# A trunk of two layers: seven products of halved blocks in the first feed-forward too, two weight sums by adding loads, and w_down steps between the products

## The chip, the cores and the metric

The kernel runs on one core of a Trainium2 chip. The core has a matrix engine (TensorE, in the profile PE, with its weight loads as PEld), VectorE (DVE), ScalarE (ACT), GpSimd (POOL) and SyncE (SP), and 16 DMA engines that all queues share. The metric is device time of one execution in microseconds; of several executions the median is given.

## The reference

A trunk of two layers over 512 latent tokens of 1024 channels, after a prefix of 256 context tokens. The even layer mixes by retention and convolution, the odd one by pooling and spatial gating; each is followed by a feed-forward. Before every part stands an RMSNorm with a shift and a scale, and behind it a gated residual; shift, scale and gate come from the vector `c` times `ada_w`. What matters here:

```python
def swiglu(h, w_gate, w_up, w_down):
    return (jax.nn.silu(h @ w_gate) * (h @ w_up)) @ w_down

D_MODEL, SEQ, DEPTH = 1024, 512, 2
D_FF = 2816            # 22 tiles of 128
# ada_w (DEPTH, 1024, 6 * 1024), ffn_w_gate and ffn_w_up (DEPTH, 1024, 2816), ffn_w_down (DEPTH, 2816, 1024)
```

All of it is float32.

## The kernel before

**Layout.** The residual stream stays in SBUF as eight tiles `xT[k]` of 128 channels x 512 tokens. A float32 product is made of three matmuls on rounded parts (`mm3`, L503): every operand is split into a high part (a rounding copy by ScalarE) and a low part (the operand minus the high part). For weights the low part is a subtraction on VectorE, or, for names in `DL`, a negated copy on ScalarE to which a DMA from GpSimd's queue then adds the operand (`low_part`, L413, `add_dma`, L327). Weight operands are 128 x 128, moving operands 512 columns (all tokens) or 256.

**First feed-forward** (`ffn`, L1596, called with layer 0). The 22 hidden tiles go in pieces of 8, 6, 4 and 4. For each four tiles `gemm` loads weights 0.5 MB at a time, splits them and makes gate and up in the straight form: per tile 8 blocks of rows x 3 matmuls of 512 columns. `gemm_acc` then adds the piece's product with w_down to `xT`, half of the output tiles at a time. The first four gate tiles are made while the norm before is still in work, and the last four rows of w_down are left to the stage that follows (`cross`, `last_of`), where they are multiplied half of the tokens at a time, so that the next norm can begin on the first half.

**Conditioning rows.** Beside the first feed-forward VectorE makes the modulation vectors of the rest: `ada` (L750) loads 0.5 MB of `ada_w`, into three buffers, and `row_dot` (L746) multiplies it with the vector and sums along the row. 56 of these are spread by `pace` over the stage, at a rate `ADA_RATE` of TensorE's time.

**Second feed-forward** (`ffn_seven`, L1762). Tiles 0 to 5 go in the straight form, tiles 6 to 21 in four groups of four. A group's gate is one product of a 1024 x 512 weight block with a 1024 x 512 block of `h`. Both are halved in both directions, and `seven` makes the four blocks of the result out of seven products instead of eight, each of 2 tiles x 4 blocks of rows x 3 = 24 matmuls of 256 columns (L1834); up is made in the same way. For that, sums of weight quarters are needed (`combine`, here four sums of two VectorE instructions in each group) and sums of quarters of `h` (`blocks`, once). The partial results lie in four PSUM banks a group: a second product is added to a bank after its first value was read by ScalarE or VectorE. High and low parts of gate times up are made by `rows_of` in tiles of the pool gp.

**Order.** In the second feed-forward the order on TensorE, VectorE and ScalarE is written out by hand: `steps` is a list, and each step's matmuls are followed by its evictions, then by the preparation of the weights that are used five steps later (`line.ahead(m + DEPTH)`), then by an entry of `filler` (the quarters of `h`, `rows_of`). An entry `(None, ...)` in `steps` puts the group's `rows_of` into `filler`. `Line` holds the weight loads in six buffers; a buffer is loaded anew on SP's queue when its last preparation was made. The product with w_down stands, for the first three groups, between the gate and the up of the group that follows, and for the last after its `(None, ...)` entry, with four output tiles at a time. In the first feed-forward the order is left to the scheduler, by priority.

Of the kernel before, what the change touches and what calls it, by code (L numbers as in the profile page):

```python
# [9 lines left out]
F32 = mybir.dt.float32  # L10
# [5 lines left out]
P = 128  # L16
D = 1024
# [12 lines left out]
ADA_RATE = 0.25  # L30
# [10 lines left out]
ACT_SLOTS = 46  # L41
# [13 lines left out]
WAY_V = ("extra", "extra", None, None)  # L55
# [12 lines left out]
PIECES = (8, 6, 4, 4)  # L68
# [3 lines left out]
FILLS = (0, 1, 1, 0, 1, 1, 1, 1, 2, 2, 2)  # L72
# [175 lines left out]
def trunk_kernel(ctx: ExitStack, tc: tile.TileContext, A, out: bass.AP):  # L248
# [104 lines left out]
    dump = const.tile([P, D], BF16, name="dump")  # L353
# [349 lines left out]
    def cross(w, k0, rhs, gate, name, order, scales, head, prep, func, end=lambda: None):  # L703

        W = [load_w(w, k0, 4, c0, 512, name) for c0 in (0, 512)]
# [38 lines left out]
    araw = [None]  # L744

    def row_dot(raw, row, dst, last=True):  # L746

        STT(out=raw if last else dump, in0=raw, scalar=1.0, in1=row, op0=ALU.mult, op1=ALU.mult, accum_out=dst)

    def ada(l, m):  # L750
# [16 lines left out]
        return [(1.2, piece(d)) for d in range(KD)]  # L767

# [37 lines left out]
    def even_start(pool):  # L806

        w_in = A["even_w_in"]

# [687 lines left out]
    def odd_layer(dpool, hx):  # L1497
# [89 lines left out]
        gemm_acc(A["odd_w_out"], 0, 4, pool_cat, mods[(1, 2)], 'oa')  # L1587
        a = scale_vec(mods[(1, 4)], 1, 1)
        sg = [slot() for _ in range(4)]
        order = [(A["ffn_w_gate"][1], 2 * b * P, 0, "f", WAY_F[b]) for b in range(4)]  # L1590
        h = cross(A["odd_w_out"], 4, sg_cat, mods[(1, 2)], 'ol', order, lambda: (a, mods[(1, 3)]),
                  lambda V, c, h: gate_half(V["f"], sg)(c, h), PREP_F, AF.Silu)
        return h, sg


    def ffn(l, begun, end):  # L1596
        wg, wu, wd = A["ffn_w_gate"][l], A["ffn_w_up"][l], A["ffn_w_down"][l]
        h, sg0 = begun
        g5 = mods[(l, 5)]
        f0 = 0  # L1600
        for nf in PIECES:
            G = []
            for fa in range(0, nf, 4):
                nt = min(4, nf - fa)
                c0 = (f0 + fa) * P
                sg = sg0 if c0 == 0 else [slot() for _ in range(nt)]

                def ev_gate(i, ps, c=slice(0, T)):
                    ACT(out=sg[i][:, c], in_=ps, func=AF.Silu)

                def ev_up(i, ps):
                    TT(out=sg[i], in0=ps, in1=sg[i], op=ALU.mult)
                    G.append(split(sg[i]))

                if c0:
                    gemm(wg, KD, c0, nt, h, ev_gate, name=f'g{l}')
                gemm(wu, KD, c0, nt, h, ev_up, name=f'u{l}' if c0 else f'v{l}')
            if f0 + nf < DFF // P:
                gemm_acc(wd, f0, nf, G, g5, f'd{l}')
            else:  # L1620
                return end(wd, f0, G, g5, f'l{l}')
            f0 += nf


    class Line:
# [4 lines left out]
        def __init__(self, pool):  # L1630
            self.pool = pool
            self.loads, self.last, self.raws = [], [], []
            self.preps, self.made, self.summed = [], [], 0
            self.q = {}

        def load(self, key, w, r0, rows, c0, cn):
            self.loads.append((key, w, r0, rows, c0, cn))
            self.last.append(None)
            return len(self.loads) - 1

        def fetch(self):

            while len(self.raws) < len(self.loads):
                n = len(self.raws)
                if n >= self.RAWS and self.last[n - self.RAWS] >= len(self.made):
                    return
                key, w, r0, rows, c0, cn = self.loads[n]
# [3 lines left out]
                nc.sync.dma_start(out=raw[:, :rows * cn].rearrange("p (k c) -> p k c", c=cn),  # L1651
                                  in_=w[r0 * P:(r0 + rows) * P, c0:c0 + cn].rearrange("(k p) c -> p k c", p=P))
                self.raws.append(raw)
                self.q[key] = [raw[:, x:x + T] for x in range(0, rows * cn, T)]

        def prep(self, key, uses, sums=None):

            n = len(self.preps)
            for u in uses:
                self.last[u] = n  # L1660
            self.preps.append((key, sums))
            return n
# [8 lines left out]
        def ahead(self, n):  # L1671

            while len(self.made) < min(n, len(self.preps)):
# [4 lines left out]
                for i, x in enumerate(src):  # L1678
                    ACT(out=hi[:, i * T:(i + 1) * T], in_=x, func=AF.Copy)
                for i, x in enumerate(src):  # L1680
                    c = slice(i * T, (i + 1) * T)
                    TT(out=lo[:, c], in0=x, in1=hi[:, c].bitcast(F32), op=ALU.subtract)
# [3 lines left out]
    def combine(a, b, op, out=None):  # L1686
        out = out or [slot() for _ in a]
        for o, x, y in zip(out, a, b):
            TT(out=o, in0=x, in1=y, op=op)
        return out  # L1690

    def blocks(h, pool):
# [16 lines left out]
        def sub(out, a, b):  # L1709
            def f():  # L1710
                o, x, y = ([t[:, :T], t[:, T:]] for t in (F[out], F[a], F[b]))
                combine(x, y, ALU.subtract, o)
# [9 lines left out]

        return B, [quarter("11", 0, n1), quarter("12", 0, n2), sub("11", "12", "11"), quarter("22", 1, n2),
                   sub("12", "22", "12"), sub("22", "22", "11"), both("t2", "22"), both("t1", "11"),
                   quarter("21", 1, n1), sub("21", "21", "22"), both("t3", "12"), both("t4", "21")]

    class Gate:
# [12 lines left out]
        def put(self, i, j, ps, sb=None):  # L1740
# [3 lines left out]
            else:  # L1744
                TT(out=o, in0=self.view(ps), in1=self.view(sb), op=ALU.add)
                self.later.append(lambda: ACT(out=o, in_=o, func=AF.Silu))

    class Up:
# [5 lines left out]
        def put(self, i, j, ps, sb=None):  # L1754
# [5 lines left out]
            TT(out=o, in0=self.g.view(ps), in1=o, op=ALU.mult)  # L1760

    def ffn_seven(l, begun, end, pool):  # L1762
# [138 lines left out]
        for nt in SEVENS:  # L1901
# [13 lines left out]
            if done:  # L1915
                down(*done)
# [152 lines left out]
```

## Time and profile before

| | us |
|---|---|
| median of 3 runs | 1129.09 |
| lowest and highest | 1128.79, 1129.55 |
| the profiled execution | 1128.8 |
| its span, from first to last instruction | 1126.8 |

The profile is that of one execution. The time of an execution is its span and what lies around it, here 2.0 us. Comparisons of a changed kernel are made with runs of the kernel before on the same chip.

### The profile page before, as it was taken

How to read it: one execution, taken by the hardware profiler on the slowest of the kernel's cores; microseconds unless marked ns; L12 is line 12 of the kernel's file. 1: busy time of each engine (PE TensorE's matmuls, PEld its weight loads, DVE VectorE, ACT ScalarE, POOL GpSimd, SP SyncE). 2: the span in 40 equal slices, each digit the busy share in tenths (PEclk: the TensorE clock that was granted, in tenths of full speed). 3: DMA queues.
4: the chain of work that ended last, by engine and by line, in shares of the span. 5: the costliest groups of instructions: out<-in, count | busy, mean ns of one | idle time of the engine just before them, and what ended most of it. 6: DMA issues, size and time to landing. Idle time of an engine off the chain costs nothing.

```text
span 1126.8 us, 15718 instructions
## 1 busy us (share of the span) xinstructions
PE 1104.3 (98%) x5978; PEld 943.8 (84%) x5978; DVE 827.0 (73%) x1472; ACT 474.5 (42%) x795; POOL 75.6 (7%) x104
## 2 busy tenths in 40 slices
PE   6999999999999999999999999999999999999997
PEld 3878876469988888888888988899889998989986
DVE  5989998998864655655653878567577886969856
ACT  5556655566522212322213543445334353524521
POOL 4012122313000000000000000000000000000000
PEclk7999999999999999999999999999999999999998
DMA  9689977569375666566534143233313252323302
GB/s 349 235 225 261 262 187 181 163 206 231 108 254 198 209 198 205 192 200 219 174 94 133 36 138 114 94 95 103 123 57 112 76 150 72 117 74 113 113 1 75
DMA packets 88827, 173.12 MB, mean 154 GB/s; under 512 B 6192, under 2 KB 31152, under 8 KB 88752
## 3 DMA queue, kind: packets, MB, share of 16 engines
q1 hardware_dynamic: 80384, 153.79, 41.5%
q0 software_dynamic: 7120, 17.02, 8.3%
q10 hardware_dynamic: 1248, 1.32, 0.4%
q8 instruction: 47, 0.77, 0.3%
q14 instruction: 28, 0.23, 0.1%
HBM read 153.00 MB, written 2.10 MB: 138 GB/s over the span
## 4 chain that ended last, share of the span: by engine, by line
PE 89%; DVE 4%; issue 2%; DMA 2%; POOL 1%; ACT 1%; POOLq 0%; DVEq 0%
PE pg L324 73%; PE pg L1834 14%; DVE a L295 3%; PE pm L324 2%; POOL s L303 1%; DVE dump L295 1%; DMA wl<-raw 1%; DMA a<-raw 1%; ACT a L309 1%; DMA x<-in_xT 0%; PE pg L1579 0%; POOL a L328 0%; DMA a<-a 0%; ACT dm L309 0%; DVE x L295 0%
## 5 line engine op out<-in xcount | busy, mean ns | idle before, releaser
L324 PE MATMUL pg<-a,wh 128*128 128x512 f32 (+1 forms) x2080 | 573.6, 362 | 0.9 <-DVE x L295 0.9
L324 PEld LDWEIGHTS pg<-a,wh 128*128 128x128 f32 x2080 | 372.9, 189 | 61.9 <-DVE x L295 1.3
L324 PE MATMUL pg<-a,wl 128*128 128x512 f32 (+1 forms) x1040 | 375.9, 362 | 0.0
L295 DVE TENSOR_TENSOR wl<-raw,wh 128x512 fp32r<-128x512 f32 (+1 forms) x231 | 200.6, 897 | 184.8 <-ACT wh L309 184.4
L309 ACT ACTIVATE wh<-raw 128x512 fp32r<-128x512 f32 (+1 forms) x247 | 192.8, 812 | 331.4 <-PE pg L324 225.1
L324 PEld LDWEIGHTS pg<-a,wl 128*128 128x128 f32 x1040 | 196.2, 189 | 30.6 <-issue 0.5
L1834 PE MATMUL pg<-a,wh 128*128 128x256 f32 x896 | 161.4, 283 | 0.0
L1834 PEld LDWEIGHTS pg<-a,wh 128*128 128x128 f32 x896 | 140.0, 192 | 0.3
L1834 PE MATMUL pg<-a,wl 128*128 128x256 f32 x448 | 126.8, 283 | 0.0
L324 PE MATMUL pg<-a,a 128*128 128x512 f32 (+2 forms) x524 | 116.7, 378 | 2.1 <-DMA a<-raw 1.4
L324 PEld LDWEIGHTS pg<-a,a 128*128 128x128 f32 x524 | 88.3, 192 | 26.4 <-issue 8.6
L295 DVE SCALAR_TENSOR_TENSOR x<-pg,mod,x 128x512 f32<-128x512 f32 (+1 forms) x140 | 84.5, 625 | 25.3 <-PE pg L324 24.7
L295 DVE TENSOR_TENSOR a<-a,a 128x256 f32<-128x256 f32 (+3 forms) x159 | 87.2, 557 | 12.3 <-ACT a L309 9.9
L1834 PEld LDWEIGHTS pg<-a,wl 128*128 128x128 f32 x448 | 86.0, 192 | 0.0
L324 PE MATMUL pg<-gp,wh 128*128 128x512 f32 (+1 forms) x320 | 83.5, 350 | 0.0
L295 DVE SCALAR_TENSOR_TENSOR ar<-ar,cbx 128x1024 f32<-128x1024 f32 (+1 forms) x70 | 81.5, 1173 | 1.9 <-DMA ar<-in_ada_wT 1.8
L295 DVE SCALAR_TENSOR_TENSOR a<-a,vec,a 128x505 f32<-128x505 f32 (+14 forms) x115 | 78.5, 739 | 0.0
L309 ACT ACTIVATE a<-pg 128x512 f32<-128x512 f32 (+2 forms) x88 | 46.7, 545 | 71.5 <-PE pg L324 58.1
L309 ACT ACTIVATE a<-a 128x512 fp32r<-128x512 f32 (+3 forms) x97 | 54.7, 576 | 50.2 <-DVE a L295 48.7
L303 POOL TENSOR_TENSOR s<-s,mhalf 128x2 f32<-128x2 f32 (+2 forms) x19 | 18.9, 994 | 797.2 <-DVE s L295 784.0
L324 PEld LDWEIGHTS pg<-gp,wh 128*128 128x128 f32 x320 | 55.8, 188 | 8.3
L324 PE MATMUL pg<-wh,a 128*128 128x512 f32 x192 | 59.8, 391 | 0.0
(135 smaller groups left out, 886.5 us busy)
## 6 DMA issues: line engine op xcount, KB each, us to landing
ar<-in_ada_wT SPq DMA_DIRECT2D x83, 512.0 KB, 4.8
raw<-in_ffn_w_gate SPq DMA_DIRECT2D x44, 512.0 KB, 3.8
raw<-in_ffn_w_up SPq DMA_DIRECT2D x44, 512.0 KB, 3.8
raw<-in_ffn_w_down SPq DMA_DIRECT2D x44, 512.0 KB, 3.6
raw<-in_even_w_in SPq DMA_DIRECT2D x24, 512.0 KB, 5.0
wl<-raw POOLq DMA_DIRECT2D x16, 512.0 KB, 6.9
a<-in_ada_wT SPq DMA_DIRECT2D x26, 256.0 KB, 5.9
raw<-in_odd_w_in SPq DMA_DIRECT2D x12, 512.0 KB, 3.7
```

The lines of the kernel that those rows point to most:

```text
L295: latest[0] = op(**kw).ins
L303: op(**kw)
L309: last_act[0] = nc.scalar.activation(**kw).ins
L324: nc.tensor.matmul(ps, L, R, start=start, stop=stop)
L1834: nc.tensor.matmul(o, x[:, s], y, start=fresh and p == k == j == 0, stop=False, skip_group_check=True)
```

## The change

The first feed-forward is made by the code of the second (now `ffn`, for both; the old `ffn` is gone). In it, and so in both stages:

- Two of the four weight sums (`s1` and `s3`) are made by the load: a plain load brings one quarter, then a DMA from GpSimd's queue adds the other from HBM onto it. Signs are turned so that all sums are additions; blocks of `h`, the Silu and the product with up take the sign back. Loads are sorted by first use.
- The order of the products is now a, c, b, d; the second eviction reads two banks.
- w_down goes two output tiles at a time (`piece`), and these four pieces stand at given places between the 14 products of the group that follows (`DOWN_AT`). The last two tiles of the straight part join the rows of the first group.
- In the first feed-forward low parts of all straight weights and of half of the w_down pieces are made by ScalarE and a DMA (`by_dma`).
- Conditioning rows have one buffer (`ada_row`): a load is issued behind the row sum that frees the buffer. 40 row sums stand in the first feed-forward (one a step for eight steps, then one every second step), 8 in the odd layer, 8 in the first eight steps of the second feed-forward.
- All eight PSUM banks serve the first feed-forward. The last w_down weights are handed to `cross` ready-made; two of the four weights that follow go into slots, with low parts by DMA.

The diff, cut to its core:

```diff
-ADA_RATE = 0.25
+ADA_RATE = 0.14
+SPLIT_ADA = 4
-ACT_SLOTS = 46
+ACT_SLOTS = 45
-WAY_V = ("extra", "extra", None, None)
+WAY_V = ("slots", "slots", None, None)
-FILLS = (0, 1, 1, 0, 1, 1, 1, 1, 2, 2, 2)
+SPARE = 2
+DOWN_AT = ((), (5, 8, 11, 14), (5, 8, 11, 14), (5, 9, 14, 14))
+DMA_EACH = 4
...
+    def ada_row(pool, which):
+        raw = pool.tile([P, D], F32, name=nm("ar"), tag="ar")
+        todo = [(l, m, d) for l, m in which for d in range(KD)]
...
+        def load(n):
+            if n < len(todo):
+                l, m, d = todo[n]
+                nc.sync.dma_start(out=raw, in_=A["ada_wT"][l, m * D + d * P:m * D + (d + 1) * P, :])
+
+        def piece(n, l, m, d):
+            def f():
+                row_dot(raw, cbx, accs[(l, m)][:, d:d + 1])
+                load(n + 1)
...
         def fetch(self):
...
+                to = raw[:, :rows * cn].rearrange("p (k c) -> p k c", c=cn)
+                nc.sync.dma_start(out=to, in_=w[r0 * P:(r0 + rows) * P, c0:c0 + cn].rearrange("(k p) c -> p k c", p=P))
+                if more:
+                    r1, c1 = more
+                    add_dma(to, w[r1 * P:(r1 + rows) * P, c1:c1 + cn].rearrange("(k p) c -> p k c", p=P))
...
         def ahead(self, n):
...
+                    if len(self.made) in self.by_dma:
+                        ACT(out=lo[:, c], in_=hi[:, c].bitcast(F32), func=AF.Copy, scale=-1.0)
+                        add_dma(lo[:, c].bitcast(F32), x)
+                    else:
+                        TT(out=lo[:, c], in0=x, in1=hi[:, c].bitcast(F32), op=ALU.subtract)
...
         def down(f0, nt, G):
-            for half in range(2):
-                def put(i, ps, half=half):
-                    d = half * 4 + i
+            def piece(d0):
+                def put(i, ps):
+                    d = d0 + i
                     STT(out=xT[d], in0=ps, scalar=g5[:, d:d + 1], in1=xT[d], op0=ALU.mult, op1=ALU.add)
-                straight(wd, f0, nt, half * T, lambda: G, put)
+                return lambda: straight(wd, f0, nt, d0 * P, lambda: G, put, 2, by_dma and d0 % DMA_EACH == 0)
+            return [piece(d0) for d0 in range(0, KD, 2)]
...
-            for x, r0, cc in (("11", 0, c0), ("21", 0, c0 + hw), ("22", 4, c0 + hw), ("12", 4, c0)):
-                load[x] = line.load(key(x), w, r0, 4, cc, hw)
+            for x, r0, cc, more in (("11", 0, c0, None), ("s1", 0, c0 + hw, (4, c0 + hw)), ("s3", 0, c0 + hw, (0, c0)),
+                                    ("12", 4, c0, None), ("22", 4, c0 + hw, None)):
+                load[x] = line.load(key(x), w, r0, 4, cc, hw, more)
             def s2():
-                q[key("s1")] = combine(q[key("21")], q[key("22")], ALU.add)
-                q[key("s2")] = combine(q[key("s1")], q[key("11")], ALU.subtract)
-            def s3():
-                q[key("s3")] = combine(q[key("11")], q[key("21")], ALU.subtract, q[key("21")])
+                q[key("s2")] = combine(q[key("s1")], q[key("11")], ALU.add, q[key("s1")])
...
             def second(ps):
                 TT(out=tmp["u"], in0=ps, in1=tmp["u"], op=ALU.add)
-            def third(ps):
                 tmp["x"] = slot()[:, cols]
-                TT(out=tmp["x"], in0=ps, in1=tmp["u"], op=ALU.add)
+                TT(out=tmp["x"], in0=acc["c"][:, cols], in1=tmp["u"], op=ALU.add)
             product("a", "11", "11", True, first, ["11"])
-            product("b", "s2", "t2", True, second, ["11", "22"], s2)
-            product("c", "s1", "t1", True, third)
+            between()
+            product("c", "s1", "t1", True, lambda ps: None, ["s1"])
+            between()
+            product("b", "s2", "t2", True, second, ["s1", "11"], s2)
...
+        for c, nt in enumerate(SEVENS):
+            gt, G = [], rest if c == 0 else []
+            todo = down(*done) if done else []
+            count = [0]
+            def between(todo=todo, count=count, at=DOWN_AT[c]):
+                count[0] += 1
+                for _ in range(at.count(count[0])):
+                    todo.pop(0)()
...
+            seven(wg, f0 * P, nt, B, new, between)
+            seven(wu, f0 * P, nt, B, lambda gt=gt: Up(gt[0]), between)
             steps.append((None, lambda gt=gt, G=G: filler.extend(rows_of(lambda: gt[0], G))))
-            if done:
-                down(*done)
...
+            start_spare()
             m = 0
             for f, after in steps:
                 if f is None:
                     after()
                     continue
+                if spare and (m < KD or m % SPARE == 0 and not filler):
+                    spare.pop(0)[1]()
                 f()
...
+    ar = ctx.enter_context(tc.tile_pool(name="ada", bufs=1))
+    banks.update(g=list(range(8)), m=list(range(BANKS_G, 8)))
+    with tc.tile_pool(name="gp", bufs=GP_BUFS) as pool:
+        hx = ffn(0, begun, to_odd, pool, ada_row(ar, [(0, 5)] + [(1, m) for m in range(SPLIT_ADA)]), True)
+    start, filler[:] = ada_row(ar, [(1, m) for m in range(SPLIT_ADA, 5)])
+    pace.update(rate=ADA_RATE, due=0.0, place=True)
+    start()
...
-        ffn_seven(1, begun, tail, pool)
+        ffn(1, begun, tail, pool, ada_row(ar, [(1, 5)]), False)
```

## Rows read from the trace of the kernel before

**Rows 1.** The page, parts 1 and 2: engines, and granted clock in 40 slices.

```profile
PE 1104.3 (98%) x5978; PEld 943.8 (84%) x5978; DVE 827.0 (73%) x1472; ACT 474.5 (42%) x795; POOL 75.6 (7%) x104
...
PEclk7999999999999999999999999999999999999998
```

**Rows 2.** The chain that ended last, in order: start us, us, what.

```profile
292.24 342.72 PE pg L324 x1618
...
884.67 40.31 PE pg L1834 x336
924.99 22.31 PE pg L324 x96
```

**Rows 3.** Windows: stretch, length; busy us of each engine; clock, DMA share, GB/s.

```profile
305.87:621.49 315.62, 315.62 (x1395) 261.26 (x1394) 177.95 (x243) 85.68 (x101) 0.00 (x0) 1.00 0.59 191
...
884.51:924.82 40.31, 40.31 (x337) 40.31 (x336) 34.64 (x56) 20.23 (x36) 0.00 (x0) 1.00 0.39 119
924.82:947.14 22.32, 22.32 (x99) 18.10 (x97) 14.37 (x22) 5.65 (x10) 0.00 (x0) 1.00 0.24 72
...
250.00:280.00 30.00, 30.00 (x219) 28.54 (x218) 26.73 (x76) 20.97 (x41) 9.36 (x11) 1.00 0.97 234
60.00:150.00 90.00, 88.63 (x392) 72.88 (x391) 82.09 (x146) 57.58 (x89) 20.00 (x24) 1.00 0.91 245
...
651.80:714.80 63.00, 63.00 (x281) 51.99 (x280) 46.17 (x97) 27.73 (x41) 4.46 (x5) 1.00 0.37 124
```

**Rows 4.** Groups by shape, TensorE, 305.87 to 621.49 us: count, busy us, mean ns.

```profile
L324 PE MATMUL pg<-a,wh 128*128 128x512 f32 x928 | 285.6, 389 | 0.0
L324 PE MATMUL pg<-a,wl 128*128 128x512 f32 x464 | 180.4, 389 | 0.0
```

**Rows 5.** The same for 924.82 to 947.14 us, a w_down stretch.

```profile
L324 PE MATMUL pg<-gp,wh 128*128 128x512 f32 x64 | 20.1, 395 | 0.0
```

**Rows 6.** Timeline of VectorE, 1086 to 1094 us: start us, us, what.

```profile
1087.35 1.29 DVE L295 TENSOR_TENSOR gp<-gp,gp 128x512 fp32r<-128x512 f32 x2 [9.63 <-ACT gp L309]
```

**Rows 7.** Timeline of TensorE, where a w_down stretch ends, twice.

```profile
884.51 0.40 PE L1834 MATMUL pg<-a,wh 128*128 128x256 f32 x2
...
1092.54 0.40 PE L324 MATMUL pg<-gp,wh 128*128 128x256 f32 x2
```

**Rows 8.** Timeline of VectorE, 883.5 to 887 us.

```profile
884.71 0.75 DVE L295 SCALAR_TENSOR_TENSOR x<-pg,mod,x 128x512 f32<-128x512 f32 x1 [0.61 <-PE pg L324]
885.38 1.28 DVE L295 TENSOR_TENSOR wl<-raw,wh 128x512 fp32r<-128x512 f32 x2
```

**Rows 9.** Groups of the whole span: a weight sum, one of four such rows.

```profile
L295 DVE TENSOR_TENSOR raw<-raw,raw 128x512 f32<-128x512 f32 x16 | 10.3, 685 | 0.0
```

**Rows 10.** Timeline of ScalarE, 297 to 300 us.

```profile
297.94 2.94 ACT L309 ACTIVATE wh<-raw 128x1024 fp32r<-128x1024 f32 x3
```

**Rows 11.** Low weight parts made by DMA, 160 to 185 us: ns or us, minimum/median/maximum.

```profile
L309 ACT ACTIVATE wl<-wh x4: 1062/1062/1064, 168.1 to 182.9; 128x1024 fp32r<-128x1024 f32 x4
...
DMA to landing us min/median/max: 4.5/5.4/7.3
```

**Rows 12.** Conditioning rows (tile ar), 306 to 621 us.

```profile
L295 DVE SCALAR_TENSOR_TENSOR ar<-ar,cbx x54: 1212/1218/1225, 305.9 to 569.3; 128x1024 f32<-128x1024 f32 x54
L295 DVE DVE_READ_ACCUMULATOR ar<-ar,cbx x54: 79/82/84, 307.0 to 570.5; 128x1 f32 x54
...
  DMA ar<-in_ada_wT: 1.8, 2
...
DMA to landing us min/median/max: 3.4/4.6/6.0
```

**Rows 13.** Conditioning rows (tile ar), 60 to 150 us.

```profile
DMA to landing us min/median/max: 4.2/5.9/8.7
```

**Rows 14.** DMA queues, 60 to 150 us: packets, MB, share of 16 engines; GpSimd's.

```profile
q0 software_dynamic: 2763, 6.59, 40.8%
```

**Rows 15.** DMA queues, 305.87 to 621.49 us; SP's.

```profile
q1 hardware_dynamic: 25327, 59.92, 58.3%
```

More of the change, by code (lines that the diff above doesn't have):

```diff
@@ L67 @@
 COLD = 3.0
-PIECES = (8, 6, 4, 4)
 SEVENS = (4, 4, 4, 4)
@@ L744, in trunk_kernel @@
     araw = [None]
+    dump = [None]
     def row_dot(raw, row, dst, last=True):
-        STT(out=raw if last else dump, in0=raw, scalar=1.0, in1=row, op0=ALU.mult, op1=ALU.mult, accum_out=dst)
+        STT(out=raw if last else dump[0], in0=raw, scalar=1.0, in1=row, op0=ALU.mult, op1=ALU.mult, accum_out=dst)
     def ada(l, m):
@@ L1590, in odd_layer @@
         order = [(A["ffn_w_gate"][1], 2 * b * P, 0, "f", WAY_F[b]) for b in range(4)]
-        h = cross(A["odd_w_out"], 4, sg_cat, mods[(1, 2)], 'ol', order, lambda: (a, mods[(1, 3)]),
+        W = [load_w(A["odd_w_out"], 4, 4, c0, 512, 'ol') for c0 in (0, 512)]
+        h = cross(W, sg_cat, mods[(1, 2)], order, lambda: (a, mods[(1, 3)]),
                   lambda V, c, h: gate_half(V["f"], sg)(c, h), PREP_F, AF.Silu)
         return h, sg
[L1596 to L1622, printed above, removed]
     class Line:
@@ L1631, in __init__, with load, begin @@
             self.pool = pool
-            self.loads, self.last, self.raws = [], [], []
+            self.loads, self.uses, self.raws = [], [], []
             self.preps, self.made, self.summed = [], [], 0
+            self.by_dma = set()
             self.q = {}
-        def load(self, key, w, r0, rows, c0, cn):
-            self.loads.append((key, w, r0, rows, c0, cn))
-            self.last.append(None)
+        def load(self, key, w, r0, rows, c0, cn, more=None):
+            self.loads.append((key, w, r0, rows, c0, cn, more))
+            self.uses.append([])
             return len(self.loads) - 1
+        def begin(self):
+            order = sorted(range(len(self.loads)), key=lambda n: self.uses[n][0])
+            self.loads, self.last = [self.loads[n] for n in order], [self.uses[n][-1] for n in order]
+            for n in range(self.RAWS, len(order)):
+                assert self.uses[order[n]][0] > self.last[n - self.RAWS]
+            self.fetch()
         def fetch(self):
@@ L1646, in fetch @@
                     return
-                key, w, r0, rows, c0, cn = self.loads[n]
+                key, w, r0, rows, c0, cn, more = self.loads[n]
                 own = n % self.RAWS >= 4
@@ L1745, in put @@
                 TT(out=o, in0=self.view(ps), in1=self.view(sb), op=ALU.add)
-                self.later.append(lambda: ACT(out=o, in_=o, func=AF.Silu))
+                self.later.append(lambda: ACT(out=o, in_=o, func=AF.Silu, scale=-1.0 if i else 1.0))
     class Up:
@@ L1759, in put, with ffn @@
                 ps = t
-            TT(out=o, in0=self.g.view(ps), in1=o, op=ALU.mult)
-    def ffn_seven(l, begun, end, pool):
+            if i:
+                STT(out=o, in0=self.g.view(ps), scalar=-1.0, in1=o, op0=ALU.mult, op1=ALU.mult)
+            else:
+                TT(out=o, in0=self.g.view(ps), in1=o, op=ALU.mult)
+    def ffn(l, begun, end, pool, spare, by_dma):
         gate_of_h = list(gate)
@@ L1943, in ffn_seven @@
                     g()
-                for _ in range(FILLS[m] if m < len(FILLS) else 1):
-                    if filler:
-                        filler.pop(0)()
-            for g in later + filler:
+                if filler:
+                    filler.pop(0)()
+            for g in later + filler + [f for _, f in spare]:
                 g()
```

123 lines of the change are left out of this document (65 added, 58 removed).

## The prediction

> **What bounds the kernel now.** I read the page's engine table first: TensorE is busy for 98% of the span, VectorE for 73%, and the granted clock is full but for the first and last slice [rows 1]. Busy is not proof of a bound, so next the chain that ended last: it is nearly all matmuls, in unbroken runs, one of 342.72 us over the first feed-forward and one of 40.31 us over two groups of seven products in the second [rows 2]. The reader is to see that nothing else comes between: in both feed-forwards TensorE waits for nothing. The windows then give each stretch its length: the first feed-forward takes 315.62 us at clock 1.00 (2.4 GHz), with VectorE busy 178, ScalarE 86, GpSimd 0, and the DMA engines 59% [rows 3]. So time is won there by fewer or shorter matmuls alone, and lost by whatever makes TensorE wait.
>
> **What a matmul costs.** The first feed-forward holds 928 + 464 = 1392 matmuls of 512 columns [rows 4] in 315.62 us: 226.7 ns each. Two groups of seven products hold 336 [rows 2] of 256 columns [rows 7] in 40.31 us [rows 3]: 120.0 ns each. A 256-column one is thus dearer than half a 512-column one (113.4 ns). A third price: a down stretch whose moving operand lies in the gp tiles [rows 5] holds 96 of 512 columns [rows 2] in 22.32 us [rows 3], 232.5 ns each.
>
> **Part 1, seven products in the first feed-forward.** Of its 22 hidden tiles, 16 leave the straight form. That removes 16 x 8 x 3 x 2 = 768 matmuls of 512 columns, 174.1 us, and adds 8 groups x 168 = 1344 of 256 columns, 161.3 us: 12.9 us less, not the eighth (21.8 us) that the count of products suggests. The Trainium skill (TensorE: Matmul & The Clock Gate, section "Wait — 56ns, not 53.3ns?") puts a warm matmul at N/2.4 GHz plus about 2.5 ns; by it the gain would be an estimated 19.0 us. The trace has 13.3 ns over N/2.4 GHz at both sizes, so the sum goes by the rows. Of the w_down products, 288 now read gp tiles: 288 x 5.8 ns = 1.7 us more (nothing, if the slower reading has a cause that is not the tile; hence 0 to 1.7, taken 1.7).
>
> **Part 2, the order of w_down.** The matmuls are the same. But for the last group the new `DOWN_AT` puts two w_down steps after the seventh up product, and only behind them comes the entry that hands out `rows_of`, which makes the high and low parts that the last products read. Before, that entry stood ahead of the down steps: their low parts were written from 1087.35 us, while TensorE had down work until 1092.54 us, and TensorE went on without a gap [rows 6, 7]. That cover is gone. VectorE runs in written order: after the last down matmul come its two evictions, the first 0.2 us later (884.51 to 884.71) and the next instruction 0.67 us after that [rows 7, 8], then the first low part, 0.68 us. So TensorE waits some 0.2 + 2 x 0.67 + 0.68 = 2.2 us at the end of each feed-forward, 4.5 us in all (0 if something reorders it).
>
> **Part 3, the accumulating loads.** They take two of the four weight sums off VectorE: four of eight instructions, 2.6 us a group at 0.64 us each [rows 9]. In the second feed-forward nothing waits for VectorE, so this gains nothing there. In the first it makes room: without them a pair of groups there would need VectorE for 34.6 us of 40.31 [rows 3], with them about 29.4 us, 2.1 us a product. ScalarE stays near half busy and hides its added negations. On GpSimd's queue each such load waits for its plain load, with later ones and the low-part adds queued behind it; GpSimd has nothing else to do in that stretch [rows 3], and both are issued five products ahead, so I take 0 (more under (b)). The entry to the first feed-forward now prepares by ScalarE, ScalarE, DMA: 297.94 us [rows 10] plus two passes of 1.06, plus 4.5 us for the quickest landing or 7.3 for the slowest [rows 11], is 304.6 to 307.4 us; the first product is due at 305.87. The loads of the stage hardly begun, I take the quick end: 0 (up to 1.5).
>
> **Part 4, the conditioning rows.** Before, three buffers; now one, so a load waits for the row sum before it, and the next row sum, in VectorE's order, waits for that load. Queued behind it are weight preparation and evictions, which TensorE needs; on SP's queue the load itself stands between weight loads that follow the same order. One turn lasts the landing plus 1.3 us of row sum (1.22 and 0.08 [rows 12]). Between downs a turn is two products, 5.76 us. Landings were 4.6 us in the first feed-forward with 59% DMA and no accumulating traffic [rows 12, 3], and 5.9 us in the stretch at 91% in which the accumulating queue took 40.8% [rows 13, 14, 3]. In the first pair of groups, with no down steps between, I count 17 plain loads (8.9 MB) and 4 accumulating ones (2.1 MB). At the plain rate (59.92 MB in 58.3% of 315.62 us: 325 GB/s [rows 15]) and the accumulating one (6.59 MB in 40.8% of 90 us: 180 GB/s [rows 14]) that is 27.4 + 11.7 = 39 of 40.3 us, accumulating share 29%. Between the two ends by that share the landing is 4.6 + 1.3 x 29/40.8 = 5.5 us, a turn 6.8 us, and seven turns put VectorE 7.3 us late. How late may it be? The third product's eviction reads the second's bank, which the sixth product writes again: 5.76 us less two VectorE passes and their start, some 4.2 us. So TensorE waits about 3.1 us; at the ends 0 (4.6) and 5.9 (5.9). In the other groups down steps of 24 x 0.2267 = 5.4 us stand between and let VectorE catch up. Row sums in the middle layer (8, one every 1.2/0.14 = 8.6 us) fall into VectorE's free time there, 46.2 of 63 us busy [rows 3]; those of the second feed-forward come one to a 5.4 us step with hardly an accumulating load beside them. Both taken as 0.
>
> **The sum.** The profiled execution took 1128.8 us, 2.0 us of it outside its span; the median of the runs is 0.3 us more. 1128.8 - 12.9 + 1.7 + 4.5 + 3.1 + 0.3 = 1125.5 us. A measurement of this kernel tells about 0.2% (2.3 us) from no change.
>
> **Rivals.**
> (a) The row buffer turns slower, and TensorE pays for every turn. With landings of 5.9 us the sum is 1128.3 us; if a chunk or two with downs fall behind as well, up to 1131. For it: the first pair of groups is nearly full on the DMA engines, and ScalarE too can stand behind a late accumulating load. Against: before, VectorE waited for rows 1.8 us in 315 us [rows 12], and a late VectorE asks for less DMA.
> (b) The other side: the DMA engines become the bound. The first feed-forward will ask for 70 weight loads, 4 for the next stage and 40 rows of 0.52 MB, 59.8 MB of plain loads (184 us at 325 GB/s), 19 low parts by accumulating, 10.0 MB (55 us at 180), and 16 accumulating weight loads, 8.4 MB. No row shows an accumulating load from HBM in 1 KB pieces. At 180 GB/s all makes 286 us against TensorE's 304 us: hidden, barely. The kernel becomes slower than before by 2.3 us when the stage exceeds 313 us, that is when these loads fall under 114 GB/s; at 100 GB/s the stage is 323 us and the whole 1141 us. For it: at 97% DMA share the engines moved only 234 GB/s [rows 3]. Against: no such stretch before made TensorE wait for long.
> (c) Better: the two ends do not stall, or gp tiles are not slower, or rows land as before. Without the stalls and the waits it is 1128.8 - 12.9 + 1.7 + 0.3 = 1117.9 us; without the gp price 1116.2 us.
> (d) The gain is hidden anyway (TensorE not the bound in the first feed-forward): nothing speaks for it, 1392 matmuls fill 315.62 us exactly; no chance of its own.
>
> **How the numbers follow.** My forecast, 1122 to 1126.8 us, gets 0.42; (c), below 1122, 0.18; (a), 1126.8 to 1131.3, 0.22; (b), above, 0.18. Faster by over 0.2% is the first two, 0.60; within 0.2% is (a), 0.22; slower 0.18. The likeliest case gives 1125.5 us. The range leaves out less than a tenth on either side: the part of (c) under 1118 and that of (b) over 1134.
>
> **What would show it.** Right: 1344 matmuls of 256 columns at 120.0 ns in the first feed-forward, the stage some 8 to 12 us shorter; a gap of about 2.2 us on TensorE at the end of each feed-forward, ended by a VectorE low part; waits of VectorE for rows from HBM in the first pair of groups, and TensorE gaps ended by VectorE there of some 3 us in all. Wrong: no gap at the ends (part 2), row landings over 6 us and gaps in every group (a), ScalarE waiting for weight loads and a DMA share near 1 through the stage (b), or another matmul pitch (part 1).

## The result, and the profile after

The changed kernel takes 1161.09 us (median of 4, 1158.04 to 1164.93) against 1128.94 us for the kernel before: ratio 1.0287, 95% interval 1.0255 to 1.0318. It is 2.9% slower where 0.3% faster was forecast, and beyond the upper end of the range, 1134 us.

The page of the profiled execution (span 1158.8 us), parts 1 and 2, against [rows 1]:

```profile
PE 1107.5 (96%) x6554; PEld 966.7 (83%) x6554; DVE 866.3 (75%) x1426; ACT 516.3 (45%) x777; POOL 138.0 (12%) x158
...
PEclk9999999999999999998999999999999999999998
DMA  8789878479597679778868625450765666565502
```

TensorE's busy time grew by 3 us and the span by 32, so TensorE waits now. The windows (columns as in [rows 3]), in the order of the lines: the first feed-forward; the second without its end, and its end; the middle layer:

```profile
309.03:650.75 341.72, 312.89 (x1970) 283.15 (x1969) 227.18 (x299) 133.15 (x167) 37.43 (x35) 0.98 0.81 215
...
817.63:1110.98 293.35, 293.35 (x1923) 269.49 (x1922) 208.81 (x249) 112.49 (x136) 20.61 (x16) 1.00 0.59 153
1110.98:1123.74 12.76, 11.32 (x50) 8.87 (x48) 7.40 (x10) 4.42 (x6) 0.00 (x0) 1.00 0.00 1
650.75:817.63 166.88, 166.77 (x1029) 149.82 (x1029) 131.20 (x271) 75.19 (x133) 9.03 (x10) 1.00 0.40 124
```

Where the 32.0 us went: the first feed-forward begins at 309.03 us instead of 305.87 (+3.2) and lasts 341.72 us instead of 315.62 (+26.1); the second lasts 306.11 instead of 304.42 (+1.7); the rest is +1.0. So the loss lies where the gain was forecast. Its 341.72 us are 312.89 busy and 28.83 idle. The waits of TensorE there (who waited for whom: us, times, longest):

```profile
PE pg L1867 <- DVE a L297: 12.5, 5, 5.6
PE pg L326 <- DMA wl<-raw: 11.6, 4, 8.4
PE pg L326 <- DVE gp L297: 4.5, 2, 3.1
```

They are late evictions (VectorE's reads of finished PSUM banks), late low parts that come by an adding DMA, and late parts of gate times up. Behind them stands VectorE. Its own longest waits, and those of SP's queue, in the same stretch:

```profile
DVE ar L297 <- DMA ar<-in_ada_wT: 77.4, 19, 13.7
```

```profile
SPq L782 <- DVE ar L297: 88.0, 25, 8.6
SPq L1661 <- DMA wl<-raw: 66.7, 14, 11.0
```

The landing of the conditioning rows (tile `ar`), and the queues (SP's and GpSimd's: packets, MB, share of 16 engines):

```profile
DMA to landing us min/median/max: 3.2/4.7/13.4
```

```profile
q1 hardware_dynamic: 39218, 55.06, 49.5%
q0 software_dynamic: 11530, 18.07, 30.8%
```

Before, VectorE waited 1.8 us for rows, and GpSimd issued nothing there [rows 12, 3]. How one such wait becomes TensorE's longest, by the chain that ended last (start us, us, what):

```profile
495.07 9.87 DMA ar<-in_ada_wT
...
504.96 1.25 DVE ar L297 x2
...
513.72 1.15 DVE wl L297
...
514.89 4.56 DMA raw<-in_ffn_w_up
...
520.75 9.35 DMA wl<-raw
...
531.42 6.85 DMA ar<-in_ada_wT
```

and by the timelines of GpSimd, then TensorE (start, us, what, idle before):

```profile
520.00 1.28 POOL L330 DMA_DIRECT2D raw<-in_ffn_w_up  x1 [25.63 <-DVE raw L297]
520.75 1.45 POOL L330 DMA_DIRECT2D wl<-raw  x1
```

```profile
530.14 0.79 PE L326 MATMUL pg<-gp,wl 128*128 128x512 f32 x1 [8.39 <-DMA wl<-raw]
```

A row takes 9.87 us to land; VectorE, in written order, makes the next weights' low parts late; that frees a raw buffer (one of the six that weights are loaded into) late, so a plain load is issued late (514.89); the adding load that waits for it is at the head of GpSimd's queue. The low part that TensorE needs next stands behind it: its negated copy was ready at 515.71 us, its adding transfer was issued at 520.75, 5.0 us later, and then took 9.35 us itself. TensorE stands for 8.39 us.

The chain goes on: the next row lands only 6.85 us after 531.42. Its buffer was free at 524.41, but on SP's queue a weight load stood ahead of it that waited for that same adding low part to land, until 530.10. The longest of VectorE's waits, 13.7 us, came about in the same way: the row's buffer was free at 346.32 us, and its load was issued at 353.34, behind a weight load that had waited 11.0 us for an adding low part. So two of the 19 awaited rows were held back by 7.0 us each before they were issued, and a third by 2.1 us.

The ends of the two feed-forwards show the gap that was forecast, 1.44 us each. The timelines of TensorE and VectorE at the first:

```profile
650.75 0.50 PE L326 MATMUL pg<-gp,wh 128*128 128x256 f32 x2 [1.44 <-DVE gp L297]
```

```profile
649.35 0.75 DVE L297 SCALAR_TENSOR_TENSOR x<-pg,mod,x 128x512 f32<-128x512 f32 x1 [0.56 <-PE pg L326]
650.01 2.49 DVE L297 TENSOR_TENSOR gp<-gp,gp 128x512 fp32r<-128x512 f32 x4
```

And the entry, by the chain and TensorE's timeline: the first low part by DMA lands at 312.17 us, and TensorE waits 2.55 us for it.

```profile
303.87 8.30 DMA wl<-raw
...
312.21 2.80 PE pg L326 x11
```

```profile
312.21 0.50 PE L326 MATMUL pg<-a,wl 128*128 128x512 f32 x1 [2.55 <-DMA wl<-raw]
```

### The profile page after: what moved, and what is told of

Read it like the earlier page. It is cut to its first block, busy times and chain, and to the rows that moved or that the text cites. A ratio compares the mean times of both kernels' runs of the same rounds, so it can differ in the third digit from the quotient of the medians.

```text
span 1158.8 us, 17040 instructions
## 1 busy us (share of the span) xinstructions
PE 1107.5 (96%) x6554; PEld 966.7 (83%) x6554; DVE 866.3 (75%) x1426; ACT 516.3 (45%) x777; POOL 138.0 (12%) x158
## 4 chain that ended last, share of the span: by engine, by line
PE 67%; DMA 15%; DVE 10%; issue 4%; ACT 3%; POOL 1%; SPq 0%; POOLq 0%; DVEq 0%; ACTq 0%
PE pg L326 48%; PE pg L1867 17%; DMA ar<-in_ada_wT 8%; DVE a L297 3%; DMA wl<-raw 3%; DVE wl L297 2%; DVE ar L297 2%; PE pm L326 2%; ACT a L311 2%; ACT wh L311 1%; DVE raw L297 1%; DMA raw<-in_ffn_w_up 1%; DMA x<-a 1%; DVE gp L297 1%; DMA a<-raw 1%
## 5 line engine op out<-in xcount | busy, mean ns | idle before, releaser
L311 ACT ACTIVATE wh<-raw 128x1024 fp32r<-128x1024 f32 (+1 forms) x219 | 224.7, 1040 | 356.3 <-DVE raw L297 141.1
L1867 PE MATMUL pg<-a,wh 128*128 128x256 f32 x1792 | 326.3, 285 | 12.5 <-DVE a L297 12.5
L326 PE MATMUL pg<-a,wh 128*128 128x512 f32 (+1 forms) x1248 | 334.6, 356 | 1.3 <-DVE x L297 1.2
L297 DVE TENSOR_TENSOR wl<-raw,wh 128x1024 fp32r<-128x1024 f32 (+1 forms) x185 | 221.8, 1203 | 80.3 <-ACT wh L311 79.2
L1867 PE MATMUL pg<-a,wl 128*128 128x256 f32 x896 | 254.8, 284 | 0.2 <-DVE wl L297 0.2
L326 PE MATMUL pg<-a,wl 128*128 128x512 f32 (+1 forms) x624 | 221.6, 355 | 2.8 <-DMA wl<-raw 2.8
L326 PE MATMUL pg<-gp,wh 128*128 128x512 f32 (+1 forms) x640 | 169.2, 354 | 6.0 <-DVE gp L297 6.0
L326 PEld LDWEIGHTS pg<-gp,wh 128*128 128x128 f32 x640 | 112.3, 191 | 23.1 <-DVE gp L297 3.8
L326 PE MATMUL pg<-gp,wl 128*128 128x512 f32 (+1 forms) x320 | 113.5, 355 | 8.9 <-DMA wl<-raw 8.9
L326 PEld LDWEIGHTS pg<-gp,wl 128*128 128x128 f32 x320 | 61.0, 191 | 18.3 <-DMA wl<-raw 9.7
L297 DVE TENSOR_TENSOR a<-pg,a 128x512 f32<-128x512 f32 x80 | 54.7, 687 | 28.5 <-PE pg L326 19.6
```

Source lines behind the costliest of these rows:

```text
L297: latest[0] = op(**kw).ins
L311: last_act[0] = nc.scalar.activation(**kw).ins
L326: nc.tensor.matmul(ps, L, R, start=start, stop=stop)
L1867: nc.tensor.matmul(o, x[:, s], y, start=fresh and p == k == j == 0, stop=False, skip_group_check=True)
```

## The experiments

**Theory A**: the single row buffer gives a row too little time to land; VectorE waits, and what is queued behind it is late. **Theory B**: the adding transfers make the weights late by themselves, and the rows are a symptom. **Theory C**: a row load that waits at the head of SP's queue holds back the weight loads behind it. "Stage" is the first feed-forward; idle is TensorE's, and the last column VectorE's wait for rows with its count, both by the waits in the stage.

| run | us | ratio to before, 95% interval | stage | idle | rows awaited |
|---|---|---|---|---|---|
| changed kernel | 1161.09 | 1.0287 (1.0255-1.0318) | 341.7 | 28.8 | 77.4 (19) |
| e1 | 1128.06 | 0.9986 (0.9976-0.9996) | 306.9 | 1.9 | - |
| e2 | 1184.35 | 1.0486 (1.0449-1.0523) | 353.3 | 36.0 | - |
| e3 | 1131.04 | 1.0012 (1.0001-1.0023) | 313.7 | 7.3 | 39.3 (17) |
| e4 | 1136.30 | 1.0060 (1.0042-1.0079) | 315.4 | 7.2 | 28.2 (16) |
| e5 | 1138.85 | 1.0084 (1.0066-1.0101) | 313.9 | 6.7 | 19.6 (6) |
| e6 | 1128.25 | 0.9991 (0.9981-1.0001) | 314.2 | 6.5 | 38.7 (16) |
| e7 | 1124.73 | 0.9957 (0.9944-0.9969) | 304.5 | 0.0 | 6.0 (4) |
| e8 | 1124.88 | 0.9960 (0.9947-0.9972) | 308.1 | 3.2 | 11.9 (9) |
| e9 | 1132.99 | 1.0037 (1.0020-1.0053) | 311.6 | 5.0 | 36.1 (21) |
| e10 | 1126.43 | 0.9969 (0.9958-0.9980) | 305.4 | 0.5 | 7.7 (8) |
| e11 | 1143.21 | 1.0118 (1.0102-1.0133) | 323.1 | 12.1 | 57.8 (20) |
| e12 | 1159.63 | 1.0271 (1.0245-1.0296) | 333.2 | 19.1 | 62.6 (28) |
| e13 | 1136.08 | 1.0077 (1.0047-1.0107) | 317.0 | 8.1 | 25.1 (6) |
| e14 | 1122.37 | 0.9944 (0.9929-0.9959) | 306.8 | 1.9 | 12.5 (10) |
| e15 | 1120.92 | 0.9924 (0.9910-0.9939) | 306.0 | 1.1 | 8.2 (10) |
| e16 | 1151.93 | 1.0202 (1.0187-1.0218) | 335.2 | 20.3 | 63.8 (19) |

### Rows out, rows unread

e1 (e2 keeps the last removed line):

```diff
-                row_dot(raw, cbx, accs[(l, m)][:, d:d + 1])
+                STT(out=seen, in0=cbx, scalar=1.0, in1=cbx, op0=ALU.mult, op1=ALU.mult, accum_out=accs[(l, m)][:, d:d + 1])
-                load(n + 1)
```

> The changed kernel (1161 us), with the loads of the 56 conditioning rows behind the first feed-forward's start left out: each row sum multiplies a constant tile with itself, so VectorE does the same work but waits for no row, and 21 MB less cross the DMA engines in the stage. Left out of the computation: those modulation vectors. Theory A (VectorE stands behind rows in one buffer, and TensorE pays for it and for the lower clock after each wait): nearly all of the 26 us of TensorE's waits and 8 us of low clock in the stage go, 1127 to 1133 us. Theory B (the DMA engines are too full with accumulating traffic; weights come late, the rows are a symptom): part of it stays, 1138 to 1150 us.

> As the run without rows, but every row is still loaded (same bytes, same queue, one behind each row sum) into a tile that no row sum reads. Left out: the modulation vectors. Theory A: only the waiting mattered, 1127 to 1134 us, within 2 us of the run without rows. Theory B: the traffic mattered, 1148 to 1160 us.

e1 came out as A has it: all accumulating traffic stayed, and the stage fell to 306.9 us. (The rows' own traffic went with the waiting, so e1 alone does not tell the two apart.) But e2 is slower than the changed kernel, against A and beyond B. Its SP queue tells why:

```profile
SPq L783 <- DMA ar<-in_ada_wT: 150.5, 38, 8.2
```

With no row sum to pace it, each row load waited on SP's queue for the one before to land, and the weight loads stood behind. So e2 did not isolate the waiting: it showed that theory C's mechanism exists where row loads are not paced. Where they are, SP's waits behind row sums need not cost TensorE anything: they come to 88.0 us in the changed kernel's stage, to 96.8 us in e8's and to 85.7 us in e7's, and TensorE waits 28.8, 3.2 and 0.0 us there.

### Less accumulating traffic

e3: `by_dma` is False for the first feed-forward. e16: only its straight steps.

```diff
-            straight(wu, 0, KD, c0, lambda: h, ev_up, nt, by_dma)
+            straight(wu, 0, KD, c0, lambda: h, ev_up, nt)
...
-        straight(wg, 0, KD, 4 * P, lambda: h, ev_gate, 2, by_dma)
+        straight(wg, 0, KD, 4 * P, lambda: h, ev_gate, 2)
```

e4: four plain loads and sums by VectorE, in both feed-forwards. e8: e3 and e4.

```diff
+            def s1():
+                q[key("s1")] = combine(q[key("21")], q[key("22")], ALU.add, [slot(), slot()])
+            def s3():
+                q[key("s3")] = combine(q[key("21")], q[key("11")], ALU.add, q[key("21")])
```

> The changed kernel with the low parts of the first feed-forward's straight weights and w_down pieces made by VectorE (no negated copies, no accumulating DMA for them; 10 MB less accumulating traffic, 19 x 1.2 = 23 us more work for VectorE in the stage). Theory A: the entry wait of 3.2 us goes, rows land sooner, but every row is still awaited; 1143 to 1153 us. Theory B: most of the loss goes, 1130 to 1142 us.

> The changed kernel with the two weight sums made by VectorE again in both feed-forwards (four plain loads of 0.5 MB for seven products instead of five plain and two accumulating; two sums of 1.3 us more on VectorE for seven products). Theory A: rows land sooner, but VectorE has 2.5 us more per seven products and the same waits; 1145 to 1157 us. Theory B: three tenths of the traffic of those stretches goes, 1132 to 1145 us.

> The changed kernel without any of the new accumulating traffic: low parts in the first feed-forward and both weight sums in both made by VectorE, rows still one by one in one buffer. If the accumulating traffic is what stretches the landings and VectorE has the room (about 35 of 40 us in a pair of groups): 1120 to 1127 us. If one row buffer is too slow by itself, or VectorE becomes the bound of the first feed-forward: 1128 to 1138 us.

> The changed kernel with the low parts of the first feed-forward's straight weights by VectorE, those of w_down by accumulating DMA as they are. If the late entry (5 us against the kernel before) comes of accumulating low parts in the straight steps: the stage begins at 306 to 308 us instead of 312, the rest of it is as long as it was; 1152 to 1158 us. If the entry is late for another reason: 1159 to 1163 us.

e3 and e4 both came out in B's range. Each takes about half of the accumulating traffic away (9.4 and 9.5 of 18.1 MB are left), gives VectorE more work, and wins 30 and 25 us; waits for rows fall to about a half and a third, and are not gone. With all of it gone (e8, in the lower of its two ranges), rows land sooner than in the kernel before [rows 12]:

```profile
DMA to landing us min/median/max: 3.2/3.7/5.5
```

VectorE, though busy for 269 of 308 us there, is not the bound. e16, at the edge of its first range, begins the stage at 306.4 us without a wait: the straight low parts are what made the entry late (but for the 1.6 us named under Open). The stage is 6.5 us shorter, 2.6 of them that wait; VectorE still waits 63.8 us for rows in it.

e11: is it the addition? The second quarter is written over the first:

```diff
-                    add_dma(to, w[r1 * P:(r1 + rows) * P, c1:c1 + cn].rearrange("(k p) c -> p k c", p=P))
+                    nc.gpsimd.dma_start(out=to, in_=w[r1 * P:(r1 + rows) * P, c1:c1 + cn].rearrange("(k p) c -> p k c", p=P))
```

> The changed kernel with the second load of a weight sum written over the first quarter instead of added to it: same queue, bytes, packets and waits, no addition. Left out: the sums s1 and s3. If adding is what makes these packets dear (0.41 us for 4 KB in the changed kernel's stage against 0.20 on SP's queue), rows land sooner and it comes near the run with sums by VectorE less VectorE's work, 1131 to 1140 us. If it is the bytes, the small packets or GpSimd's queue, nothing changes, 1156 to 1165 us.

At 1143.21 us it lies between both expectations, nearer the first: 19 of the stage's 37 us over its work (341.7 - 304.5, by e7 below) come back. The queues from 820 to 1100 us (packets, MB, share of 16 engines), SP's and GpSimd's in the changed kernel, then GpSimd's in e11; GpSimd's carries these 16 loads alone:

```profile
q1 hardware_dynamic: 31771, 34.95, 40.2%
q0 software_dynamic: 8448, 8.39, 20.1%
```

```profile
q0 software_dynamic: 2304, 8.39, 9.5%
```

Adding takes 56.3 us of the engines' time (149 GB/s), writing the same bytes 26.6 us (315 GB/s), in about a quarter of the packets; so the packets were not the same, as the expectation has it (and its 0.41 us for 4 KB is 0.38 us by the stage's rows). The smaller packets alone do not explain it: SP's plain loads, 1.1 KB a packet on average, ran at 310 GB/s in the same stretch.

### More time for a row to land

e13 changes only how often a row sum comes (and leaves 8 rows out):

```diff
-SPARE = 2
+SPARE = 3
...
-                if spare and (m < KD or m % SPARE == 0 and not filler):
+                if spare and (m < KD or m % SPARE == 1 and not filler):
```

e12 and e5 load halves of rows into a ring of two or three half buffers, one half a step (e5 with 44 slots):

```diff
+        raws = [pool.tile([P, T], F32, name=nm("ar"), tag=f"ar{i}") for i in range(3)]
...
+                row_dot(raws[n % 3], cbx[:, i * T:(i + 1) * T], acc[:, d, i:i + 1])
+                load(n + 3)
```

> The changed kernel, its rows loaded in halves of 256 KB into a ring of three half-size buffers (6 KB of a partition instead of 4, one activation slot fewer), one half a step instead of a whole row every second step: a half now has nearly three steps to land instead of two less a row sum. The accumulating traffic, the bytes and SP's queue stay; each load still stands behind the row sum that frees its buffer. Theory A (the one whole-row buffer turns too slowly whenever accumulating transfers stretch a landing; VectorE waits and what is queued behind it is late): VectorE's waits for rows of 72 us fall under 15, 1127 to 1136 us. Theory B (the accumulating transfers themselves come late for the weights, the rows are a symptom) and theory C (the row load that waits at the head of SP's queue holds back the weight loads behind it): 1148 to 1162 us.

> The changed kernel with rows in halves in a ring of two half buffers, so that neither memory nor the activation slots differ from it: the same bytes stay in flight, one half a step. A half has 5.0 us to land. Theory A: VectorE waits for rows at the landings above that only, 25 to 45 us in the stage instead of 72, and the start is as early as in the changed kernel: 1134 to 1146 us. Theory B or C: 1155 to 1163 us.

> The changed kernel with one row sum every third step instead of every second behind the first eight, 32 rows in the first feed-forward instead of 40; memory, slots, queue and accumulating transfers as they are. Left out: one modulation vector (8 rows; another stands in for it). A row now has 8.64 - 1.3 = 7.3 us to land where it had 4.5. Theory A (a landing longer than the time given makes VectorE wait): few landings of the changed kernel are over 7.3 us, waits for rows fall from 72 to 15 to 30 us, the stage from 338 to 312 to 320 us, 1133 to 1143 us. If not the time given but the transfers themselves matter: 8 rows less of 73 MB, 1152 to 1160 us.

VectorE's waits in the stage, e5, e12 and e13:

```profile
DVE ar L297 <- DMA ar<-in_ada_wT: 19.6, 6, 13.0
```

```profile
DVE ar L297 <- DMA ar<-in_ada_wT: 62.6, 28, 13.6
```

```profile
DVE ar L297 <- DMA ar<-in_ada_wT: 25.1, 6, 14.5
```

e13 came out in A's range. e5 missed A's numbers by a little (19.6 us of waits where under 15 was expected, 1138.85 us where 1136 was the upper end) and is far from B's. Both keep the accumulating traffic, and their stages are 24.7 and 27.8 us shorter than the changed kernel's. What that traffic costs TensorE with rows nearly on time is seen in e5: 6.7 us of waits, 3.7 of them for low parts by DMA. e12 missed A's numbers and came out in B's and C's range; the landings say why that is no case against A. By issue and landing of each: of the changed kernel's 37, 20 took over the 4.46 us that a row has (two products less its sum), and of its 19 awaited rows 17 are among these; of e12's 73 halves 34 took over their 5.0 us, and 28 were awaited, since half the bytes land no sooner (median 4.8 us) among the adding packets; of e5's 72 only 6 took over 7.9 us, and 6 were awaited. e5's total is held up elsewhere: in the runs with 44 slots the stage begins at 311.5 us or later.

### The ends, and the best of it

e6 is e3 with the entry first; e14 is e8 with it:

```diff
-DOWN_AT = ((), (5, 8, 11, 14), (5, 8, 11, 14), (5, 9, 14, 14))
+DOWN_AT = ((), (5, 8, 11, 14), (5, 8, 11, 14), (5, 9))
...
+                steps.append((None, lambda gt=gt, G=G: filler.append(lambda: [g() for g in rows_of(lambda: gt[0], G)])))
+                for f in todo:
+                    f()
```

> The run with low parts by VectorE (1131 us), and in both feed-forwards the entry that hands out the last group's high and low parts now stands ahead of the last two w_down steps, both halves in one go. If the order costs what the gap at each end shows (1.4 us of TensorE's wait, twice): 1127.5 to 1129 us. If the wait is only moved, 1130.5 to 1131.5 us.

> The run without new accumulating traffic (1124.9 us), with the entry ahead of the last two w_down steps in both feed-forwards; rows whole, one buffer, all slots. Without the gaps of 1.4 us at both ends: 1121 to 1123 us, the fastest so far. If the ends cost nothing: 1124.5 to 1125.5 us.

Both as expected: 2.8 us for e6 against e3, 2.5 for e14 against e8. In e6 both gaps are gone; in e14 0.4 us is left of the first.

e7 is e6 with three half buffers (44 slots), e9 with two; e10 is e9 with sums by VectorE; e15 is e14 with two half buffers in the first feed-forward alone.

> The last run and the ring of half buffers together. Theory A: the remaining waits of 5.8 us for late evictions go as well, TensorE runs through the first feed-forward at 304 to 306 us: 1119 to 1124 us, faster than both kernels. Theories B and C: no further gain, 1127 to 1130 us.

> The run with low parts by VectorE, the entry ahead of the last two w_down steps and rows in halves, but with a ring of two half buffers and all 45 activation slots. The run with three and 44 slots had a first feed-forward of 304.5 us without a wait, and began it at 311.5 us, some 5 us late from the even layer on. If the missing slot cost those 5 us and two halves turn fast enough without accumulating low parts (a half has two steps less a half row sum, 5.0 us, and landed in 4.2 us): 1118.5 to 1121.5 us. If two halves turn too slowly: 1122 to 1127 us.

> The same with the two weight sums by VectorE. If the order of the ends and the ring take away the 1.4 us at each end and the remaining wait of 1.8 us of the run without accumulating traffic (1124.9 us): 1119 to 1121.5 us. If VectorE is too full: 1122 to 1126 us.

> The last one with rows in two halves in the first feed-forward alone, whole rows after it. In the run with halves everywhere (1126.4 us) the first feed-forward was 304.9 us long with one wait of 0.5 us, and the middle layer had waits of 4.2 us that the runs with whole rows there do not have. If those waits come of two halves following each other there: 1119.5 to 1122.5 us. If they come of something else: 1124 to 1127 us.

e7's and e15's stages:

```profile
311.53:616.01 304.48, 304.48 (x1970) 278.45 (x1969) 252.90 (x411) 120.18 (x149) 24.10 (x20) 1.00 0.78 214
```

```profile
307.41:613.45 306.04, 304.94 (x1970) 278.55 (x1969) 272.10 (x467) 120.18 (x165) 3.50 (x4) 1.00 0.55 169
```

e7 has no wait in the stage at all, with the adding loads of its weight sums in place; its total lies 0.7 us over A's range. e9 missed both its ranges: VectorE waits 36.1 us for rows there, so two halves turn too slowly beside adding loads. e10 missed both as well, by 4.9 us the one that it argued for; halves that follow each other closely in the middle layer made TensorE wait 4.2 us there in its profile. e15 keeps whole rows there, has no such wait, came out in the range that this cause gave it, and is the fastest by median, 0.76% under the kernel before (its interval overlaps e14's). That is the gain of the change without its accumulating weight loads, with its ends in order and with rows in halves.

## Why the prediction was wrong

**Part 1 held.** By the chain, 456 matmuls of 256 columns in a row took 54.71 us in the second feed-forward, 120.0 ns each; in e7's first feed-forward, where nothing waits, 456 in a row took the same 54.71 us:

```profile
883.12 54.71 PE pg L1867 x456
```

```profile
377.00 54.71 PE pg L1869 x456
```

And the stage's work came out at 304.48 us (e7) where 315.62 - 12.9 + 1.7 = 304.4 was forecast. By the Trainium skill (TensorE: Matmul & The Clock Gate, section "Wait — 56ns, not 53.3ns?") the products would have given an estimated 19.0 us before the dearer w_down; the measured 11.1 us, that price included, bear the rows out.

**Part 2: right mechanism, 1.4 us an end instead of 2.2.** Only one eviction stands behind the last matmul, not two, and it starts at once: the matmul ended at 650.75 - 1.44 = 649.31 us, the eviction began at 649.35, the next instruction 0.66 us later, and the first of four low parts took 2.49 / 4 = 0.62.

**Part 3 failed where it took 0 twice.** At the entry the plan took the quick landing; the first of the adding transfers took 8.3 us instead of 4.5 to 7.3 (e3 and e16, without them at the entry, begin at 306.5 and 306.4). Others followed it by 2 us each, but that is not all of it: its first packet came 3.8 us after its issue, where those of [rows 11] that found the queue empty began after 1.4 us; why is not shown. In the stage the queueing on GpSimd, named and put at nothing because all is issued five products ahead, makes 5.0 us of the lateness behind the 8.39 us wait above: five products of lead hold only while VectorE is on time.

**Part 4 is the step that failed most.** It said that TensorE waits 3.1 us in the first pair of groups and that down steps let VectorE catch up elsewhere. In the first pair TensorE waited 11.4 us, 50.69 less the 39.29 that it was busy, and in the later groups 13.4 us where 0 was taken:

```profile
377.19:427.88 50.69, 39.29 (x313) 38.77 (x312) 38.81 (x51) 17.99 (x22) 5.16 (x4) 0.96 0.74 192
```

The mean landing was right (5.5 forecast for the first pair; 5.4 over the stage's 37), its use was not: the landings spread from 3.2 to 13.4 us, a row sum that waits holds all of VectorE's queue, and a short landing afterwards gives nothing back. So the waits added up over every group: 77.4 us on VectorE, 22.7 of them already in the straight steps ahead of the first pair. The cost should have been taken from the share of landings over 4.46 us. The part also named the row's place between weight loads on SP's queue and gave it no price; there weight loads that waited for adding low parts held rows back by 7.0, 7.0 and 2.1 us. Rival (a) had the right place and kind, with waits in all groups, but by mean landings reached only 1131.

**Rival (b), the engines' total, was not it alone.** The stage moved 73.1 MB by both queues at a share of 0.81, 277 us where 286 were forecast for 78.2 MB, and adding loads ran at 149 GB/s, above the 114 that would decide. Yet either half of the accumulating traffic had to go, or the rows had to get more time (e3, e4, e5, e13): it is both together, and neither alone, that cost 25 to 28 us of the stage. The share passes 1.0 only in parts of the stage: 1.05 from 312.21 to 340 us, where TensorE did not wait, and 1.09 from 565 to 574 us. Plain rows landed later while adding packets were in flight (median 3.7 us in e8, 4.7 here). The Trainium skill (DMA: Bandwidth & Descriptors, section "Queues, rings and completion order") has each DMA engine go round its queues packet by packet; the later landings fit that, and no run here shows the order of the packets.

**Not in the sum: the clock.** 312.89 busy us hold 304.5 us of work. Some 6 of the 8.4 us lie behind the four longest waits (5.6, 4.2, 8.4 and 3.1 us), where the granted clock was in part the lower level of 1.2 GHz (each length times what its clock, third from the end, lacks of 1):

```profile
397.33:405.00 7.67, 7.67 (x53) 7.67 (x54) 3.99 (x6) 0.00 (x0) 0.00 (x0) 0.81 0.75 233
...
427.88:434.00 6.12, 6.12 (x40) 6.12 (x41) 5.48 (x6) 2.96 (x3) 0.00 (x0) 0.75 0.53 169
...
530.14:536.00 5.86, 5.86 (x19) 4.69 (x20) 0.00 (x0) 0.00 (x0) 1.13 (x1) 0.73 0.78 262
...
577.09:583.00 5.91, 5.91 (x19) 4.68 (x20) 5.84 (x8) 2.00 (x2) 0.00 (x0) 0.71 0.58 188
```

Most of the rest are the last matmuls ahead of each of the twelve waits, which the profile counts as busy 0.1 to 0.3 us longer than in an unbroken run. The Trainium skill (the same TensorE page, section "HAM oscillation — how this bites in real kernels") warns of the lower clock behind waits on DMA; this trace agrees, at some 6 us for 28.8 us of idle time.

**Open.** How much of the loss the shared SP queue made: no run has rows on another queue. Why the first low part's packets began late at the entry. Why one slot less delays the even layer was not followed. Of the 3.2 us later begin, 1.6 us are there after 393 matmuls, 200 us ahead of any changed feed-forward, and the profiles of the other runs scatter from 106.9 to 110.4 us at that point (before 108.3, changed 109.9).

## What to carry to other kernels

A load into a single buffer, awaited by an engine that runs in written order, is priced by how many of its landings exceed the time it is given, not by the mean (e13 left the median landing at 4.8 us and gave 7.3 us: 6 waits instead of 19, for 27 rows instead of 37); and what is queued behind the wait, on that engine and on the queues that it releases, belongs to the price, as does what stands ahead of the load on its own queue. Work moved from an idle-enough VectorE to the DMA engines was a loss here: VectorE at 87% of the stage (e8) cost less than adding packets that delay everything else in flight. When a long unbroken run of matmuls starts to wait, add what it is busy longer, most of it at the lower clock: here 0.3 us for each us of idle time, in e12 and e16 0.5 (314.1 and 314.9 us busy).

## What was not expected of the hardware

- An adding load from HBM costs twice the engines' time of a plain one from the same queue (56.3 against 26.6 us for 8.39 MB) and comes in packets of 1 KB on average where the plain one has 3.6 KB (8448 packets against 2304). SP's plain packets of 1.1 KB ran at 310 GB/s beside them, so it is not the size alone.
- A load of 256 KB landed no sooner than one of 512 KB under that traffic: medians 4.8 (e12) and 4.7 us.
- The low parts by adding transfer landed later in this stage than those of the kernel before from 160 to 185 us: 4.3/7.9/11.0 us (minimum, median, maximum) against 4.5/5.4/7.3 [rows 11].
